# A convolution and attention trunk: the softmax statistics of the attention's second stage on ScalarE's DMA queue, and another order at its end

## Chip, core and metric

The kernel runs on one core of a Trainium2 chip. Its engines work in parallel, each through its own list of instructions in order: TensorE (PE in the profile, its weight loads PEld), VectorE (DVE), ScalarE (ACT), GpSimd (POOL) and SyncE (SP). SP, POOL and ACT can each start DMA transfers. The metric is the time of one execution on the device in microseconds (us); lower is better.

## What is computed

The reference is a trunk of two layers on an input of 1024 tokens by 1024 features, in float32. The first layer is a gated short convolution, the second an attention with three groups per head, dilated by 1, 4 and 16:

```
h = rms_norm(x, g);  proj = h @ w_in
for g, (window, dilation) in enumerate(((128, 1), (512, 4), (2048, 16))):
    q, k = rms_norm of this group's queries and keys; v
    o_g, lse_g = softmax(q k^T / 8 + bias) v          # causal, within the window, in residue classes
alpha = softmax over the three groups of lse_g
o = sum_g alpha_g * o_g
x = x + (o * silu(z)) @ w_out
```

There are 16 heads of 64 features; the kernel works on them as eight head pairs (`hp`). The point that matters here is `alpha`: the three groups of a head are merged by weights that come from their softmax maxima and denominators, for each token. These statistics are small, but each group holds its tokens in another order.

## The kernel before

Earlier stages compute the convolution layer and the projections, and leave queries, keys, values and the gate in DRAM (`qkd`, `vd`, `zd`). The second stage, from line 815 on, is the attention with the output projection. In it the order of every engine is the program's own: nothing is reordered.

A unit is one head pair and one group. Groups 0 and 1 are cut into four steps each, group 2 into two, so a head pair has ten steps and the stage 80. `make` gives each step its parts: `A` (line 893) computes scores in TensorE and, on VectorE, adds the bias and takes the negated maximum (into `nl`); `E` (line 940) takes the exponentials on ScalarE and their sums (into `nl` too); `B` (line 944) transposes the result in TensorE and copies it out of PSUM (`pts`), on VectorE or ScalarE; `C` (line 953) multiplies by the values, and the last `C` of a half calls `finish`, which copies the output `O`.

The main loop (line 1214) runs step numbers `k`. A part with lag `n` belonging to step `j` runs at `k = j + n`: `A` at lag 0, `B` at 2, `C` at 4. At each `k` the lags run in the order 0, 1, 4, 3, 5 to 16, 2; then come the exponentials of step `k` (key `"exps"`), then pieces of the output projection (`extra`), then loads and splits of weights (`begins`).

The last step of each unit (`end`) carries more. `store` (line 987) writes `nl` of groups 0 and 1 to DRAM (`nld`), and in group 2 reads both back as `ml`, in group 2's order of tokens: the trip through DRAM is how the order is changed. The stores consist of pieces of 16 bytes: 1024 in one DMA for group 0, 512 in each of two for group 1; the load is two DMAs of 64 rows of 256 bytes. `weights` (line 1000) takes the common maximum and the exponents' differences on VectorE and their exponentials on ScalarE; `shares` (line 1013) gives `alpha` (`fo`); `store_shares` (line 1026) writes it to DRAM (`fd`); `spread` (line 1030) reads it back, broadcast over the 64 features of a head, into `fb` or `sqacc`, two DMAs of 256 KB for each group. `scale` (VectorE) and `add` (GpSimd) merge the outputs; `gate`, `high` and `low` multiply by the gate and split the result into two parts for exact products. Before the change `store`, `store_shares` and `spread` are all issued by GpSimd, in its one queue, with the additions of `add` between them.

The output projection of head pairs 0 to 5 runs in pieces beside later steps (`some`, line 1162), each with a PSUM bank by name: `pd`, `po`, `pt` or `ps`. Its weights are loaded by `fetch` on SP and split into two parts by `split` (ScalarE) and `split_low` (VectorE). After step 80, pair 7's merging (`spread_last`, `last`) and the remaining products of pairs 6 and 7 end the kernel; five tiles of them (`first`) are begun before pair 7's result is there.

Of the kernel before, what the change touches and what calls it, by code (L numbers as in the profile page):

```python
# [28 lines left out]
HP = H // 2  # L29
# [6 lines left out]
def trunk(ctx: ExitStack, tc: tile.TileContext, a, out):  # L36
    nc = tc.nc
# [60 lines left out]
    def spread(hf, src, pool):  # L98
        cs = slice(hf * HALF, hf * HALF + HALF)
        pb = pool.tile([P, HALF], F32, name="st", tag="st")  # L100
        for j in range(4):
            b = hf * 4 + j
            nc.tensor.transpose(pb[:, j * P:(j + 1) * P], src[:, b:b + 1].to_broadcast([P, P]), ident)
        if src is rtok:
            nc.scalar.activation(R1[:, cs], pb, AF.Copy)
        else:
            mt = ftile()
            mc = mt.rearrange("p (c q) -> p c q", q=32)
            nc.vector.transpose(mc, pb.rearrange("p (c q) -> p c q", q=32))
            nc.vector.tensor_scalar(er2[:, hf * 16:(hf + 1) * 16], mc[:, :, 0], 8.0 * EPS, None, op0=OP.mult)  # L110
# [10 lines left out]
    nld = dram.tile([HP, S, 2, 4], F32, name="nld")  # L121
# [13 lines left out]
    with tc.tile_pool(name="wq", bufs=1) as wq, tc.tile_pool(name="sle", bufs=1) as sle, \  # L135
# [11 lines left out]
        def ftile():  # L147
            t = fp.tile([P, HALF], F32, name="f", tag="f", bufs=12)
            return t
# [185 lines left out]
        with tc.tile_pool(name="rp", bufs=1, side="right") as rp, tc.tile_pool(name="cp", bufs=2, side="right") as cp, \  # L335
# [62 lines left out]
            with tc.manual_schedule(engines={mybir.EngineType.Activation}):  # L398
                ps, T = {}, {}
# [107 lines left out]
        with tc.tile_pool(name="ev", bufs=1, side="right", reuse_waits="tile") as ev, tc.tile_pool(name="xb", bufs=1, side="right", reuse_waits="tile") as xb, \  # L507
# [35 lines left out]
            WO, ps = {}, {}  # L543
# [271 lines left out]
    with tc.tile_pool(name="sp", bufs=1, space=PSUM) as sp, tc.tile_pool(name="ptp", bufs=2, space=PSUM) as ptp, \  # L815
# [34 lines left out]
        def scores():  # L850
            turns[0] += 1
            return banks[turns[0] % 3]
# [11 lines left out]
        def attention(hp, g):  # L864

            u = {}
# [120 lines left out]
            def store():  # L987

                if g == 2:
                    u["ml"] = sm.tile([P, 8, 2, 4], F32, name="ml", tag="ml", bufs=1)  # L990
                    for a, hs in enumerate((lo, up)):
                        nc.gpsimd.dma_start(u["ml"][hs], nld[hp].rearrange("(i a r) g e -> a i r g e", a=2, r=8)[a])
                elif g == 0:
                    nc.gpsimd.dma_start(nld[hp, :, 0].rearrange("(b t) e -> t b e", b=8), u["nl"])
                else:
                    for n in range(2):
                        nc.gpsimd.dma_start(nld[hp, :, 1].rearrange("(n s c) e -> n s c e", n=2, c=4)[n],
                                            u["nl"][:, 4 * n:4 * n + 4])

            def weights():  # L1000
# [29 lines left out]
            def spread(w):  # L1030
                fb = u["fb", w] = fbp.tile([P, S], F32, name="fb", tag="fb") if w else sqacc
                for s, hs in enumerate((lo, up)):
                    nc.gpsimd.dma_start(fb[hs], fd[hp, w, s][None, :].to_broadcast([64, S]))

            def scale(w):
                nc.vector.tensor_tensor(O[hp, w], O[hp, w], u["fb", w], op=OP.mult)

            def add(w):
                nc.gpsimd.tensor_tensor(O[hp, 1], O[hp, 1], O[hp, w], op=OP.add)
# [22 lines left out]
            def spread_last(hf):  # L1062

                b0, b1, b2 = (scores().rearrange("p a b -> p (a b)") for _ in range(3))
                for w in (2, 1):
                    for r in range(8):
                        for a, b in enumerate((b0, b1)):
                            hs = slice(64 * a + 32 * hf, 64 * a + 32 * hf + 32)
                            nc.tensor.transpose(b.rearrange("p (w i r) -> p w r i", w=2, r=8)[:, w - 1, r],
                                                u["wide", w][hs, r * P:r * P + P], ident[hs, hs])  # L1070
                mine = ident.rearrange("p (a h i) -> p h a i", a=2, h=2)[:, hf]
                for r in range(8):
                    nc.tensor.matmul(b2.rearrange("p (i a r) -> p r a i", a=2, r=8)[:, r],
                                     u["wide", 0][:, r * P:r * P + P], mine, start=True, stop=True)
                u["fb", 0] = b2
                for w in (2, 1):
                    u["fb", w] = [b.rearrange("p (w i r) -> p w i r", w=2, r=8)[:, w - 1] for b in (b0, b1)]
# [19 lines left out]
            steps = []  # L1097
            for q in range(2):
                for js in ([[2 * q, 2 * q + 4, 2 * q + 1, 2 * q + 5]] if g == 2 else
                           [[4 * q, 4 * q + 1], [4 * q + 2, 4 * q + 3]]):  # L1100
                    st = make(js, not steps)
                    steps.append({lag: [f] for lag, f in zip((0, LB, LC, "exps"), st)})
            end = steps[-1]
            end.setdefault(1 if g < 2 else 2 if hp < 2 else 1 if hp < HP - 2 else 0, []).append(store)
            if g == 2:
                if hp == HP - 1:
                    steps[-2][3] = steps[-2].pop(LC)
                    end[3] = end.pop(LC)
                    todo = [(2, shares), (2, wide), (3, lambda: spread_last(0)), (3, lambda: last(0, 0)),
                            (3, lambda: last(0, 1))]  # L1110
                    ending.update(turn=end.pop(LB)[0], weights=weights, spread=spread_last, last=last)
                else:

                    todo = [(2, weights), (3, shares), (3, store_shares), (4, lambda: spread(2)),
                            (4, lambda: spread(1)), (4, lambda: spread(0)), (8, lambda: scale(2)),
                            (9, lambda: scale(1)), (9, lambda: add(2)), (10, lambda: scale(0)),
                            (10, lambda: add(0)), (12, gate), (12, high), (13, low)] if hp == HP - 2 else [
                            (4 if hp < 2 else 3, weights), (5, shares), (5, store_shares), (7, lambda: spread(2)),
                            (7, lambda: spread(1)), (7, lambda: spread(0)), (10, lambda: scale(2)),
                            (11, lambda: scale(1)), (11, lambda: add(2)), (12, lambda: scale(0)),  # L1120
                            (12, lambda: add(0)), (13, gate), (14, high), (15, low)]
                for lag, f in todo:
                    end.setdefault(lag, []).append(f)
# [30 lines left out]
        def bank(name):  # L1154
            if name in ("pd", "po"):
                return (pp1 if name == "pd" else opp).tile([P, HALF], F32, name=name, tag=name)
            t = scores() if name == "ps" else ptp.tile([P, 4, P], F32, name=name, tag=name)
            return t.rearrange("p a b -> p (a b)")
# [3 lines left out]
        def some(kts, dt, hf, name):  # L1162

            ps = bank(name)
            dense(ps, kts, dt, hf, True, True)
            sums.append((ps, acc[dt][:, half(hf)]))

        def add_sums():
            while sums:
                ps, x = sums.pop(0)  # L1170
                nc.vector.tensor_tensor(x, ps, x, op=OP.add)  # L1171

        steps, at = [], {}
# [7 lines left out]
        tiles = [(dt, hf) for hf in range(2) for dt in range(KT)]  # L1181

        def when(k, f, *x):
            begins.setdefault(k, []).append(lambda: f(*x))
# [7 lines left out]
        for r in range(3):  # L1192
            k0 = at[2 * r + 2, 0][0] + LD
            k = k0
            for i, (dt, hf) in enumerate(tiles):
                late = k >= len(steps)
                name = "pd" if not late else (("pd", "ps"), ("pd", "ps"), ("pd", "pt"), ("pt", "pd"))[
                    min(k - len(steps), 3)][i % 2]
                if i >= 14:
                    name = "po"  # L1200
                extra.setdefault(k, []).append(lambda r=r, dt=dt, hf=hf, name=name:
                                               some((2 * r, 2 * r + 1), dt, hf, name))
                k += (i % 2 if i < 13 else 0) if late else 1
        for kt in range(KT):
            k = (at[kt // 2 * 2 + 2, 0][0] + 4 if kt < 6 else len(steps) - 6) + 2 * (kt % 2)
            when(k - 5 - 2 * (kt % 2), fetch, kt)
            when(k, split, kt)
            when(k + 2, split_low, kt)
# [4 lines left out]
        k = 0  # L1213
# [22 lines left out]

        last = ending["last"]
        add_sums()
        first = [(dt, hf, bank(name)) for (dt, hf), name in zip(tiles, ("pt", "pt", "po", "po", "pd"))]
        for dt, hf, ps in first:  # L1240
            dense(ps, (6,), dt, hf, True, False)
        ending["spread"](1)
        last(1, 0)
        last(0, 2)
        for dt, hf, ps in first:
            dense(ps, (7,), dt, hf, False, True)
        last(1, 1)
# [3 lines left out]
        for dt, hf, ps in first[2:]:  # L1251
            close(ps, dt, hf)
        for i, (dt, hf) in enumerate(tiles[5:]):
            ps = bank(("ps", "ps", "ps", "pt", "pt", "po", "po", "pd", "ps", "ps", "ps")[i])
            dense(ps, (6, 7), dt, hf, True, True)
            close(ps, dt, hf)

# [66 lines left out]
```

## Time and profile before

| What | Value |
|---|---|
| Median of 3 runs | 1973.18 us (1970.7 to 1974.63) |
| Profiled execution | 1968.56 us |
| Its span, first to last instruction | 1966.8 us |
| Mean granted TensorE clock | 0.991 |
| TensorE busy | 1913.9 us, 97% |
| VectorE busy | 1495.3 us, 76% |
| ScalarE busy | 886.9 us, 45% |
| GpSimd busy | 847.6 us, 43% |

The times of the profile are those of one execution. A row of the timeline gives the start, the duration, the engine, the line of the code, the operation with what it writes and reads (`out<-in`) and, in brackets, how long the engine was idle before it and what ended that. A row of waits gives who waited for whom, then the sum in us, how often, and the longest. A row of a source line gives durations in ns as min/median/max. "DMA to landing" is the time from issue until the transfer's semaphore says that the data has arrived, again as min/median/max, for the line named before it. A row of stretches gives, for each engine, the busy time in that stretch.

### The profile page before, as it was taken

The page shows a single profiled execution, that of the slowest core. Times are in us where ns is not written, and L with a number is a line of the kernel's source. Part 1 is how long each engine was busy: PE and PEld are TensorE (multiplying, and loading weights), DVE is VectorE, ACT ScalarE, POOL GpSimd, SP SyncE. Part 2 cuts the span into 40 slices and gives each one's busy share as a digit, 9 for nine tenths or more (in the row PEclk, how much of TensorE's full clock was granted, in tenths as well). Part 3 has the DMA queues.
Part 4 walks back from the last instruction along what each step waited for, and adds up shares of the span by engine and source line. Part 5 has one row for each costly group of instructions (what it writes and reads, how often), then busy time and mean ns, then how long its engine had stood idle before and what let it go on. Part 6 is the DMA issues. An engine that isn't in the chain of part 4 may idle for free. (4 is left out here: it accounts for less than half of the span.)

```text
span 1966.8 us, 30588 instructions
## 1 busy us (share of the span) xinstructions
PE 1913.9 (97%) x10894; PEld 1555.4 (79%) x10894; DVE 1495.3 (76%) x2769; ACT 886.9 (45%) x2031; POOL 847.6 (43%) x767
## 2 busy tenths in 40 slices
PE   8999999999999999999999999999999999889988
PEld 6888888888888888878878888888888876667767
DVE  7876766666666655788888689868988878878896
ACT  6433333333334444443433443343344338877770
POOL 0366667666665211333434444444344441333230
PEclk9999999999999999999999999999999999999999
DMA  6312232222224665322323232333323247897742
GB/s 198 117 58 88 87 107 76 97 80 93 81 80 143 195 230 177 119 90 91 124 97 123 81 119 96 106 110 107 105 89 118 97 163 234 244 280 229 225 124 86
DMA packets 116777, 253.79 MB, mean 129 GB/s; under 512 B 17598, under 2 KB 22814, under 8 KB 116624
## 3 DMA queue, kind: packets, MB, share of 16 engines
q1 hardware_dynamic: 93280, 176.89, 27.9%
q0 software_dynamic: 23344, 74.95, 11.3%
q8 instruction: 85, 1.39, 0.3%
q14 instruction: 68, 0.56, 0.1%
HBM read 192.53 MB, written 67.64 MB: 132 GB/s over the span
## 5 line engine op out<-in xcount | busy, mean ns | idle before, releaser
L165 DVE TENSOR_TENSOR ws<-wr,ws 128x512 fp32r<-128x512 f32 x284 | 274.4, 968 | 120.8 <-ACT ws L164 119.3
L164 ACT ACTIVATE ws<-wr 128x512 fp32r<-128x512 f32 x284 | 178.3, 629 | 356.1 <-PE pp L304 231.9
L164 ACT ACTIVATE ws<-sr 128x512 fp32r<-128x512 f32 x272 | 169.9, 629 | 295.7 <-PE pp L304 240.6
L276 POOL TENSOR_TENSOR sr<-wr 128x512 f32<-128x512 f32 x136 | 185.6, 1365 | 264.2 <-DMA wr<-in_conv_w_in 67.5
L165 DVE TENSOR_TENSOR ws<-sr,ws 128x512 fp32r<-128x512 f32 x272 | 227.0, 842 | 71.6 <-ACT ws L164 69.4
L313 DVE TENSOR_TENSOR f<-pp,f 128x512 f32<-128x512 f32 x204 | 139.7, 685 | 93.0 <-PE pp L304 86.3
L942 ACT ACTIVATE xs<-xs,nl 128x256 f32<-128x256 f32 (+2 forms) x384 | 160.5, 424 | 1.0 <-DVE nl L936 1.0
L309 ACT ACTIVATE f<-pp 128x512 f32<-128x512 f32 x228 | 132.7, 582 | 27.4 <-POOL blkc L682 12.7
L671 ACT ACTIVATE f<-f 128x512 f32<-128x512 f32 x96 | 60.7, 632 | 138.7 <-DVE f L313 102.1
L276 POOL TENSOR_TENSOR sr<-wr,sr 128x512 f32<-128x512 f32 x68 | 88.5, 1302 | 70.3 <-issue 47.4
L936 DVE CUSTOM_DVE_ANT_0 xs<-ps,bt 128x256 f32<-128x256 f32 (+2 forms) x384 | 102.5, 325 | 12.5 <-PE ps L923 7.4
L301 PE MATMUL pp<-blkg,ws 128*128 128x512 f32 x272 | 107.2, 394 | 3.2 <-ACT f L309 3.2
L301 PE MATMUL pp<-blkf,ws 128*128 128x512 f32 x272 | 108.5, 399 | 0.7 <-ACT f L309 0.7
L301 PE MATMUL pp<-blkb,ws 128*128 128x512 f32 x272 | 108.1, 398 | 0.0
L301 PE MATMUL pp<-blka,ws 128*128 128x512 f32 x272 | 107.3, 394 | 0.7 <-ACT f L309 0.7
L301 PE MATMUL pp<-blkd,ws 128*128 128x512 f32 x272 | 106.9, 393 | 0.0
L304 PE MATMUL pp<-blkb,ws 128*128 128x512 f32 x272 | 106.6, 392 | 0.0
L303 PE MATMUL pp<-blkb,ws 128*128 128x512 f32 x272 | 106.5, 392 | 0.0
L304 PE MATMUL pp<-blkf,ws 128*128 128x512 f32 x272 | 106.3, 391 | 0.0
L276 POOL TENSOR_TENSOR sr<-sr,wr 128x512 f32<-128x512 f32 x68 | 104.0, 1529 | 4.9
L304 PE MATMUL pp<-blkd,ws 128*128 128x512 f32 x272 | 106.0, 390 | 0.0
L304 PE MATMUL pp<-blka,ws 128*128 128x512 f32 x272 | 106.0, 390 | 0.0
(341 smaller groups left out, 5280.5 us busy)
## 6 DMA issues: line engine op xcount, KB each, us to landing
wr<-in_conv_w_in SPq DMA_DIRECT2D x128, 256.0 KB, 3.1
wr<-in_wqk SPq DMA_DIRECT2D x96, 256.0 KB, 3.1
qkd<-blkc POOLq DMA_DIRECT2D x48, 512.0 KB, 3.4
qk<-qkd SPq DMA_DIRECT2D x48, 512.0 KB, 5.2
wr<-in_conv_w_out SPq DMA_DIRECT2D x64, 256.0 KB, 3.1
f<-in_x SPq DMA_DIRECT2D x48, 256.0 KB, 4.4
wr<-in_wv SPq DMA_DIRECT2D x48, 256.0 KB, 3.2
vd<-f POOLq DMA_DIRECT2D x48, 256.0 KB, 2.6
```

Of the source, the lines that this page charges most:

```text
L164: nc.scalar.activation(t[:, 0], src, AF.Copy)
L165: nc.vector.tensor_tensor(t[:, 1], src, t[:, 0].bitcast(F32), op=OP.subtract)
L276: nc.gpsimd.tensor_tensor(t, x, y, op=op)
L301: nc.tensor.matmul(ps, w[:, 0, ws], b[:, k, 0], start=new and k == 0, stop=False, skip_group_check=not new)
L303: nc.tensor.matmul(ps, w[:, 0, ws], b[:, k, 1], start=False, stop=False, skip_group_check=not new)
L304: nc.tensor.matmul(ps, w[:, 1, ws], b[:, k, 0], start=False, stop=end and k == 3, skip_group_check=not new)
L309: nc.scalar.activation(t, ps, AF.Copy)
L313: nc.vector.tensor_tensor(m, ps, m, op=OP.add)
L671: nc.scalar.activation(sq, t, AF.Square)
L936: nc.vector.tensor_tensor_reduce(out=x, in0=flat[s][:, cols], in1=u["bt"][s][:, bs], op0=OP.add, op1=OP.min, scale=-1.0, scalar=3e38, accu ...
L942: nc.scalar.activation(x, x, AF.Exp, bias=nm, scale=-1.0, accum_out=L)
```

## The change

Four things change. In `store` all DMAs go from GpSimd's queue to ScalarE's. `store` itself moves from lags 0 to 2 of the unit's last step to the place right behind that step's exponentials. In head pairs 0 and 1 `weights`, `shares`, `store_shares` and `spread` come one step earlier; in head pair 6 the scalings, the additions and the gate come one step earlier. At the end, the late pieces of the output projection use other banks, the last two weight rows are fetched and split two steps earlier, the five tiles begun first use the banks in another order, and the subtraction for the first half of pair 7, `last(0, 2)`, stands ahead of `last(1, 0)`.

```diff
                 if g == 2:
                     u["ml"] = sm.tile([P, 8, 2, 4], F32, name="ml", tag="ml", bufs=1)
                     for a, hs in enumerate((lo, up)):
-                        nc.gpsimd.dma_start(u["ml"][hs], nld[hp].rearrange("(i a r) g e -> a i r g e", a=2, r=8)[a])
+                        nc.scalar.dma_start(u["ml"][hs], nld[hp].rearrange("(i a r) g e -> a i r g e", a=2, r=8)[a])
                 elif g == 0:
-                    nc.gpsimd.dma_start(nld[hp, :, 0].rearrange("(b t) e -> t b e", b=8), u["nl"])
+                    nc.scalar.dma_start(nld[hp, :, 0].rearrange("(b t) e -> t b e", b=8), u["nl"])
                 else:
                     for n in range(2):
-                        nc.gpsimd.dma_start(nld[hp, :, 1].rearrange("(n s c) e -> n s c e", n=2, c=4)[n],
+                        nc.scalar.dma_start(nld[hp, :, 1].rearrange("(n s c) e -> n s c e", n=2, c=4)[n],
                                             u["nl"][:, 4 * n:4 * n + 4])
...
-            end.setdefault(1 if g < 2 else 2 if hp < 2 else 1 if hp < HP - 2 else 0, []).append(store)
+            end["exps"].append(store)
...
+                    w = 4 if hp < 2 else 5
                     todo = [(2, weights), (3, shares), (3, store_shares), (4, lambda: spread(2)),
-                            (4, lambda: spread(1)), (4, lambda: spread(0)), (8, lambda: scale(2)),
-                            (9, lambda: scale(1)), (9, lambda: add(2)), (10, lambda: scale(0)),
-                            (10, lambda: add(0)), (12, gate), (12, high), (13, low)] if hp == HP - 2 else [
-                            (4 if hp < 2 else 3, weights), (5, shares), (5, store_shares), (7, lambda: spread(2)),
-                            (7, lambda: spread(1)), (7, lambda: spread(0)), (10, lambda: scale(2)),
+                            (4, lambda: spread(1)), (4, lambda: spread(0)), (7, lambda: scale(2)),
+                            (8, lambda: scale(1)), (8, lambda: add(2)), (9, lambda: scale(0)),
+                            (9, lambda: add(0)), (11, gate), (12, high), (13, low)] if hp == HP - 2 else [
+                            (3, weights), (w, shares), (w, store_shares), (w + 2, lambda: spread(2)),
+                            (w + 2, lambda: spread(1)), (w + 2, lambda: spread(0)), (10, lambda: scale(2)),
...
-                name = "pd" if not late else (("pd", "ps"), ("pd", "ps"), ("pd", "pt"), ("pt", "pd"))[
-                    min(k - len(steps), 3)][i % 2]
-                if i >= 14:
-                    name = "po"
+                name = "pd"
+                if late:
+                    name = {5: "ps", 7: "ps", 9: "pt", 10: "pt", 11: "po", 12: "po", 14: "pt", 15: "pt"}.get(i, "pd")
...
-            k = (at[kt // 2 * 2 + 2, 0][0] + 4 if kt < 6 else len(steps) - 6) + 2 * (kt % 2)
+            k = (at[kt // 2 * 2 + 2, 0][0] + 4 if kt < 6 else len(steps) - 8) + 2 * (kt % 2)
...
-        first = [(dt, hf, bank(name)) for (dt, hf), name in zip(tiles, ("pt", "pt", "po", "po", "pd"))]
+        first = [(dt, hf, bank(name)) for (dt, hf), name in zip(tiles, ("po", "po", "pd", "pt", "pt"))]
         for dt, hf, ps in first:
             dense(ps, (6,), dt, hf, True, False)
         ending["spread"](1)
+        last(0, 2)
         last(1, 0)
-        last(0, 2)
...
-            ps = bank(("ps", "ps", "ps", "pt", "pt", "po", "po", "pd", "ps", "ps", "ps")[i])
+            ps = bank(("ps", "ps", "ps", "po", "po", "pd", "pt", "pt", "ps", "ps", "ps")[i])
```

## The prediction

> **What bounds the kernel now.** I read the page first, then, in the attention's second stage (from 1627 us, where the first score matmul starts, to the end), the waits of TensorE, its timeline with the idle time in brackets, the timelines of VectorE (DVE), GpSimd (POOL) and ScalarE (ACT) around each hole, and the busy time by stretch.
>
> ```profile
> span 1966.8 us, 30588 instructions
> PE 1913.9 (97%) x10894; PEld 1555.4 (79%) x10894; DVE 1495.3 (76%) x2769; ACT 886.9 (45%) x2031; POOL 847.6 (43%) x767
> ...
> PE pt L949 <- DVE pts L860: 16.0, 9, 5.5
> ...
> PE pd L1135 <- DVE acc L1171: 2.5, 2, 1.5
> ...
> PE pt L1136 <- DVE qk L1095: 1.1, 1, 1.1
> ```
>
> TensorE is the bound, and all that the change touches is holes of a few microseconds in the last 340. The largest group, 16.0 us, is transposes that wait for DVE to empty a PSUM bank (`pts`). The holes, one by one, are the next rows; the number in brackets is the idle time.
>
> ```profile
> 1681.28 0.44 PE L949 MATMUL pt<-ident,xs 128*128 128x128 f32 x2 [2.43 <-DVE pts L860]
> ...
> 1685.26 0.44 PE L949 MATMUL pt<-ident,xs 128*128 128x128 f32 x2 [1.16 <-DVE pts L860]
> ...
> 1689.86 0.90 PE L949 MATMUL pt<-ident,xs 128*128 128x128 f32 x3 [0.67 <-DVE pts L860]
> ...
> 1729.62 1.12 PE L949 MATMUL pt<-ident,xs 128*128 128x128 f32 x4 [5.53 <-DVE pts L860]
> ...
> 1908.38 0.50 PE L1135 MATMUL pd<-y,y 128*128 128x512 f32 x1 [1.55 <-DVE acc L1171]
> ...
> 1928.02 0.50 PE L1135 MATMUL pd<-y,y 128*128 128x512 f32 x1 [0.99 <-DVE acc L1171]
> ...
> 1942.93 0.54 PE L1136 MATMUL pt<-qk,y 128*128 128x512 f32 x1 [1.09 <-DVE qk L1095]
> ```
>
> DVE was late because it, working in order, itself stood still:
>
> ```profile
> 1679.39 1.23 DVE L1036 TENSOR_TENSOR o<-o,fb 128x1024 f32<-128x1024 f32 x1 [2.11 <-DMA fb<-fd]
> ...
> 1683.64 1.23 DVE L1036 TENSOR_TENSOR o<-o,fb 128x1024 f32<-128x1024 f32 x1 [1.31 <-DMA fb<-fd]
> ...
> 1688.24 1.23 DVE L1036 TENSOR_TENSOR o<-o,sqacc 128x1024 f32<-128x1024 f32 x1 [1.07 <-DMA sqacc<-fd]
> ...
> 1697.78 0.17 DVE L1006 TENSOR_TENSOR mx<-ml 128x16 f32<-128x16 f32 x1 [0.89 <-DMA ml<-nld]
> ...
> 1726.66 0.79 DVE L1006 TENSOR_TENSOR mx<-ml 128x16 f32<-128x16 f32 x1 [4.63 <-DMA ml<-nld]
> ...
> 1896.03 1.22 DVE L1149 TENSOR_TENSOR y<-wraw,y 128x1024 fp32r<-128x1024 f32 x1
> ...
> 1904.71 3.02 DVE L1149 TENSOR_TENSOR y<-wraw,y 128x1024 fp32r<-128x1024 f32 x1
> ```
>
> So head pair 0 waits for its spread shares, pairs 1 and 2 for `ml`. Why these land late is in POOL's queue:
>
> ```profile
> 1671.62 2.09 POOL L1033 DMA_DIRECT2D fb<-fd  x4 [4.21 <-PE po L970]
> ...
> 1674.72 1.56 POOL L997 DMA_DIRECT2D nld<-nl  x2
> ...
> 1691.91 1.08 POOL L992 DMA_DIRECT2D ml<-nld  x2
> ...
> 1712.03 0.73 POOL L997 DMA_DIRECT2D nld<-nl  x1 [1.62 <-ACT xs L942]
> ...
> 1721.54 1.08 POOL L992 DMA_DIRECT2D ml<-nld  x2 [8.79 <-DMA nld<-nl]
> 1722.62 4.79 POOL L1039 TENSOR_TENSOR o<-o 128x1024 f32<-128x1024 f32 x2
> ...
> 1904.27 2.37 POOL L1039 TENSOR_TENSOR o<-o 128x1024 f32<-128x1024 f32 x1 [1.25 <-DVE o L1036]
> ```
>
> The 8 KB store of group 1's maxima stands in one queue behind 1.5 MB of spread shares; POOL sits 8.79 us on its landing and can neither load `ml` nor add. The last two rows also show that DVE's L1149 took 3.02 in place of 1.22 us, until POOL's addition ended (1904.27 + 2.37).
>
> **Issues on ACT.** Per head pair five DMAs move from POOL to ACT, each right behind the exponentials that fill `nl`. Whoever issues on ACT holds the exponentials and bank copies queued behind. No DMA is issued on ACT before the change, so SP's rows bound it.
>
> ```profile
> L879 SPq DMA_DIRECT2D bt<-sk x32: 319/320/1340, 1605.3 to 1860.4; - x32
> ...
> L877 SPq DMA_DIRECT2D bt<-sk x32: 444/506/1367, 1625.4 to 1871.0; - x32
> ...
> 1631.00:1682.00 51.00, 45.81 (x715) 34.68 (x708) 41.66 (x223) 48.41 (x213) 10.38 (x16) 1.00 0.78 242
> 1682.00:1719.00 37.00, 30.70 (x442) 22.47 (x436) 32.59 (x139) 29.30 (x116) 12.62 (x15) 0.91 0.86 244
> 1719.00:1757.00 38.00, 31.65 (x404) 24.53 (x404) 27.77 (x118) 27.52 (x113) 12.83 (x16) 0.91 0.89 262
> 1757.00:1795.00 38.00, 37.98 (x468) 29.09 (x467) 35.29 (x135) 29.83 (x116) 12.90 (x16) 1.00 0.95 290
> ```
>
> Of one kind: 0.32 us at least (L879, 128 rows of 1 KB); 0.506 us for small scattered rows (L877, 64 of 256 B), the nearest to these stores, so I take it. In the first stretch, head pairs 0 and 1, ACT is busy 48.41 of 51 us (the columns: busy time of PE, weight load, DVE, ACT and POOL with counts, granted clock, DMA share, GB/s): eight issues there cost 8 x 0.506 = **+4.0**. Bounds: 0 (8 x 0.32 = 2.6, the whole of ACT's 2.6 idle); and, if the time grows with the pieces, 0.32 us / 128 = 2.5 ns each: a group-0 store of 1024 pieces 2.56 us, the two group-1 stores of 512 pieces 1.28 each, so 2 x 5.1 + 2 x 0.5 = +11.2. Later ACT idles 8 to 10 us in each 37 to 38 us, and the issues (2.5 us, at most 6.1 per pair) lie in it: 0, with the bounds -1 (POOL is free of them) and +3 (a copy late for its bank).
>
> **The added wait.** ACT must not issue `ml` before both stores of group 1 have landed; POOL bore this wait so far.
>
> ```profile
> L997 POOL DMA_DIRECT2D nld<-nl x16: 709/737/889, 1644.2 to 1902.3; - x16
> ...
> DMA to landing us min/median/max: 2.5/7.6/13.7
> 1674.32 0.19 ACT L942 ACTIVATION_READ_ACCUMULATOR xs<-xs,nl 128x1 f32 x1
> ...
> 1680.58 0.19 ACT L942 ACTIVATION_READ_ACCUMULATOR xs<-xs,nl 128x1 f32 x1
> ...
> 1718.28 0.20 ACT L942 ACTIVATION_READ_ACCUMULATOR xs<-xs,nl 128x1 f32 x1
> ml<-nld POOLq DMA_DIRECT2D x16, 16.0 KB, 4.6
> ```
>
> From the last exponential of pair 1's group 1 (1674.5) to that of its group 2 (1680.8) are 6.3 us. A landing of 7.6 us, the median on POOL's queue, leaves ACT 1.3 us to wait: twice, in pairs 0 and 1, **+2.6**. Bounds: 0 (2.5 us, the fastest landing), and 13.7 - 6.3 = 7.4 for pair 1, the rival below.
>
> The Trainium skill, "DMA: Bandwidth & Descriptors", section "Issuing engines are not separate DMA queues", speaks against the change: all issuers run on the same 16 engines, and another issuer saves only the time of issuing. The same page's "Queues, rings and completion order" says that each DMA engine takes turns between the queues' rings, packet by packet, which lets a store on an empty ring pass the spread shares. The 8.79 us of the POOL row above do not tell them apart, since store and shares were in one ring; by the first it is rival 3 and 1977.9, by the second the sum below holds, 1966.5.
>
> **What goes.** *Pair 0* (shares and spread one step earlier): DVE's waits of 2.11, 1.31 and 1.07 us add up to a lateness of 4.5. Steps last about 2.5 us there (51 us for 20), so some 2 us remain; of the 4.3 us of TensorE's three holes 2.3 go, and pair 1's 0.89 with an `ml` that is issued at 1682 and not at 1691: -3.2, and with a little of the half clock below **-3.5**; bounds -5.1 and -1. More than 4.4 isn't there: DVE's idle time in the second stretch (37 less 32.59), which is late next. *Pair 2*: pair 1's spread, a step earlier too, is out of the way by some 3 us, so the store from 1712 lands in about 6, `ml` goes at 1718.5, lands 4.6 later at 1723, and DVE, ready at 1722.0, waits 1 us instead of 4.63. POOL's additions (1722.62) no longer queue behind `ml`, so `mx` takes 0.2 and not 0.79 us. Of 5.53 us, 4.3 go; the bounds are -5.5 and 0. After such holes the granted clock (third figure from the right) was half:
>
> ```profile
> 1728.30:1735.00 6.70, 5.33 (x32) 4.37 (x32) 6.60 (x27) 4.10 (x11) 1.01 (x2) 0.50 0.54 171
> ...
> 1943.30:1946.60 3.30, 3.30 (x9) 2.60 (x8) 3.23 (x6) 0.63 (x1) 0.00 (x0) 0.50 0.06 24
> ```
>
> In the first of these DVE was the busier, so only 1 us of the half-clock time counts (0 to 3.3): pair 2 **-5.3**. Pairs 3 to 6 keep their lags: 0.
>
> *The end.* The splits of the last two weight rows two steps earlier take L1149 out of POOL's way: the hole of 1.55 goes. Their 1.22 us now share a step with pair 6's first scaling, which is also moved; SP's two `wraw` loads go two steps earlier past `bt` and `qk` loads, at no cost while those are prefetched. The late tiles' other banks remove the 0.99 (the second use of `pd` waits for an addition; `po` is free by then). The subtraction for the first half ahead of `last(1, 0)` removes the 1.09, and with it perhaps half-clock time, 3.3 / 2 = 1.65. Together 5.3; since the moved splits meet a full DVE I take **-4.5** (bounds -5.3 and -2).
>
> **Sum:** 4.0 + 2.6 - 3.5 - 5.3 - 4.5 = **-6.7 us**. The profiled execution took 1968.56 us (its span 1966.8); the median of the runs is 1973.18, 4.6 above it. From the median: **1966.5 us**; a profiled execution like the one shown would take 1961.9.
>
> **Rivals.**
> 1. *All is hidden* (0.15). The stores land in 2.5 us, ACT's idle time takes the issues: 0 - 5.1 - 5.5 - 3.3 - 5.3 = -19.2, 1954.0. For it: ACT idles 8 us and more in all later stretches. Against: not in the first.
> 2. *The pieces cost ACT time* (0.17): +11.2 in place of 4.0, so 0.5: 1973.7. For it: 1024 pieces of 16 B; against: L877 with half the rows takes longer than L879, so rows don't set it.
> 3. *Slower: ACT is blocked by the landing* (0.16). The shares still fill the DMA engines, stores on ACT's queue land in 13.7 us, the maximum on POOL's; in pair 1 ACT waits 7.4 in place of 1.3 (+6.1), in pair 2 `ml` comes as late as before (+5.3): -6.7 + 11.4 = +4.7, 1977.9. It decides from a landing of about 11 us: 3.4 us more than 7.6, counted in both pairs, use up the 6.7. For it: the DMA share is 0.78 to 0.95 in the stretches above. Against: pair 0's and 1's shares start a step earlier.
> 4. *It does not do what it says* (0.10): pairs 0 to 2 wait as long for their loads as before, so only the issues and the end stay: 4.0 - 4.5 = -0.5, 1972.7; with ACT's waits (+2.6) 1975.3.
>
> **Chances.** Forecast 0.42 (faster 0.36, same 0.06), rival 1 faster 0.15, rival 2 same 0.13 and slower 0.04, rival 3 slower 0.12 and same 0.04, rival 4 same 0.10: faster by over 0.2% (3.9 us, about what a measurement of this kernel can tell from no change) 0.51, same 0.33, slower 0.16. The range leaves out the far half of rival 1 and the worst of rivals 2 and 3: 1957 to 1978.
>
> **What would show it.** Issues on ACT: rows L992, L994 and L997 of ACT's queue near 0.5 us (over 1.2: rival 2). The wait: `ml`'s landing and ACT's idle time before the copies at about 1681 (over 4 us: rival 3). Pair 2: `mx` waiting 1 us or less. The end: no L1149 of 3 us and none of its three holes. Holes of TensorE on ACT before 1682 that sum to over 7 us would make the forecast wrong.

## The result: slower

| Kernel | Median of the runs | Lowest to highest | Ratio to before, 95% interval |
|---|---|---|---|
| before | 1973.06 us (6 runs) | 1966.59 to 1975.64 | |
| after | 1982.34 us (6 runs) | 1980.9 to 1988.24 | 1.0055 (1.0036 to 1.0073) |

The change costs 9.3 us where 6.7 us of gain were forecast, and the time lies above the range. The profiled execution after took 1988.24 us, the slowest of its six. Its page, the span, the busy time and the DMA queues (packets, MB, share of 16 engines):

```profile
span 1986.5 us, 30521 instructions
...
PE 1914.1 (96%) x10894; PEld 1554.9 (78%) x10894; DVE 1501.2 (76%) x2769; ACT 886.4 (45%) x2031; POOL 817.5 (41%) x727
...
q1 hardware_dynamic: 93280, 176.89, 27.7%
q0 software_dynamic: 22064, 74.42, 11.0%
q10 hardware_dynamic: 18048, 0.53, 0.6%
```

TensorE does the same work (1914.1 against 1913.9 us); what grew is its idle time. The changed stage alone, from its first score matmul to the end (TensorE's busy time is the third figure), before and then after:

```profile
1627.16:1966.80 339.64, 305.93 (x3729) 235.16 (x3728) 280.66 (x1075) 228.89 (x905) 94.18 (x112) 0.95 0.68 205
```

```profile
1630.95:1986.50 355.55, 305.79 (x3729) 235.34 (x3728) 274.74 (x1075) 227.70 (x905) 66.36 (x72) 0.94 0.67 195
```

The stage is 15.9 us longer, all of it idle time; 3.8 us more were lost ahead of it, where the program is the same. These 19.7 us between two profiled executions are twice the 9.3 us between the medians: the rows below show where the changed kernel loses in a long execution, and the medians say how much. `q10` is new: ScalarE's queue, with 0.53 MB in 18048 packets, 29 bytes each on average. Whom TensorE waits for, first before, then after, in the waits from 1623 us to the end (sum, times, longest):

```profile
PE pt L949 <- ACT pts L862: 2.1, 5, 0.5
```

```profile
PE pt L949 <- ACT pts L862: 27.2, 9, 10.4
PE pt L949 <- DVE pts L860: 8.7, 7, 3.8
```

The 16.0 us on VectorE's copies shrank to 8.7, and 27.2 us on ScalarE's copies came in their place. In TensorE's timeline after, these are four holes, in pairs 0, 1, 2 and 3:

```profile
1663.44 0.69 PE L949 MATMUL pt<-ident,xs 128*128 128x128 f32 x2 [3.58 <-ACT pts L862]
...
1702.35 1.12 PE L949 MATMUL pt<-ident,xs 128*128 128x128 f32 x4 [10.44 <-ACT pts L862]
...
1740.97 0.69 PE L949 MATMUL pt<-ident,xs 128*128 128x128 f32 x2 [4.00 <-ACT pts L862]
...
1784.17 1.11 PE L949 MATMUL pt<-ident,xs 128*128 128x128 f32 x4 [6.94 <-ACT pts L862]
```

ScalarE's timeline around the second of them shows why the copy is late:

```profile
1691.69 0.19 ACT L942 ACTIVATION_READ_ACCUMULATOR xs<-xs,nl 128x1 f32 x1
1700.71 1.15 ACTq L992 DMA_DIRECT2D ml<-nld  x2
1701.91 0.38 ACT L862 ACTIVATE pts<-pt 128x256 f32<-128x256 f32 x1 [10.03 <-issue]
```

Its last exponential of group 2 ends at 1691.9; then ScalarE stands 8.8 us in front of the load of `ml`, issues it, and only then makes the copy for which TensorE waits. The stores that it waits for, by their source line in the trace (ns of the issue as min/median/max; landing in us the same way):

```profile
L997 ACTq DMA_DIRECT2D nld<-nl x16: 552/570/617, 1650.7 to 1927.6; - x16
...
DMA to landing us min/median/max: 2.8/10.0/15.8
```

The longest, 15.8 us, is pair 1's second store, issued at 1684.9: it landed at 1700.7, when ScalarE went on. So rival 3 happened, in pair 1 at least. (In pair 3 the last store had landed at 1779.8, and ScalarE issued the second load of `ml` only at 1783.2; the experiments come to that.) By the trace the first packet of pair 1's two stores moved at 1688.6, 5.7 us after the first of them was issued; with longer pieces, in the run long_pieces below, it was 5.1 us, so the pieces are not the reason for this part, and what is stays open. The queues in the two microseconds before 1698 (packets, MB, share) show what the store met:

```profile
q1 hardware_dynamic: 242, 0.76, 97.9%
q10 hardware_dynamic: 242, 0.00, 7.4%
```

As many packets of SyncE's loads (3 KB on average) as of the store (16 bytes): that is what engines that take turns give, and a store of 512 pieces of 16 bytes then needs 512 turns over the 16 engines. The Trainium skill, "DMA: Bandwidth & Descriptors", section "Queues, rings and completion order", gives a turn a whole packet of typically 9 to 17 descriptors; of the turns the trace agrees, of the size it does not: here every piece is a packet of its own, 242 against 242.

### The profile page after: what moved, and what is told of

Read it like the earlier page. It is cut to its first block, busy times and chain, and to the rows that moved or that the text cites. A ratio compares the mean times of both kernels' runs of the same rounds, so it can differ in the third digit from the quotient of the medians.

```text
span 1986.5 us, 30521 instructions
## 1 busy us (share of the span) xinstructions
PE 1914.1 (96%) x10894; PEld 1554.9 (78%) x10894; DVE 1501.2 (76%) x2769; ACT 886.4 (45%) x2031; POOL 817.5 (41%) x727
## 2 busy tenths in 40 slices
DMA packets 133544, 253.78 MB, mean 128 GB/s; under 512 B 35006, under 2 KB 39582, under 8 KB 133392
## 3 DMA queue, kind: packets, MB, share of 16 engines
q10 hardware_dynamic: 18048, 0.53, 0.6%
## 5 line engine op out<-in xcount | busy, mean ns | idle before, releaser
L165 DVE TENSOR_TENSOR ws<-wr,ws 128x512 fp32r<-128x512 f32 x284 | 284.7, 1004 | 119.4 <-ACT ws L164 117.6
L949 PE MATMUL pt<-ident,xs 128*128 128x128 f32 x496 | 79.8, 295 | 37.0 <-ACT pts L862 27.2
```

The costliest lines, as they stand in the source:

```text
L165: nc.vector.tensor_tensor(t[:, 1], src, t[:, 0].bitcast(F32), op=OP.subtract)
L949: nc.tensor.transpose(pt[:, i], xs[s][:, c[i][0]], ident)
```

## Experiments

Each ran beside the kernel before on the same chip, in three sessions of four: the first four of the table, the next four, and the last three with nine. The kernel before had a median of 1973.0 us (28 runs), 1973.1 (12) and 1971.1 (29) in them, so runs of different sessions are compared by their ratio to it. The twelfth, nine, ran once, for its trace (1986.13 us, with 7 MB of loads put in at its start).

| Run | What differs | Median, us | Lowest to highest | Ratio to before, 95% |
|---|---|---|---|---|
| all_pool | after, stores and `ml` on GpSimd | 1964.42 | 1963.89 to 1968.41 | 0.995 to 0.9976 |
| ml_pool | after, `ml` alone on GpSimd | 1978.29 | 1975.08 to 1984.37 | 1.0022 to 1.0045 |
| long_pieces | after, long pieces | 1976.16 | 1973.66 to 1981.6 | 1.0015 to 1.0034 |
| end_only | before with the new end | 1966.49 | 1961.49 to 1971.15 | 0.9955 to 0.9977 |
| ml_act | after, stores on GpSimd | 1981.73 | 1977.19 to 1984.65 | 1.0032 to 1.0057 |
| dup_short | all_pool, stores once more on ScalarE | 1978.93 | 1976.06 to 1983.9 | 1.0019 to 1.0044 |
| ml_pool_long | ml_pool with long pieces | 1963.51 | 1961.99 to 1965.61 | 0.9943 to 0.9968 |
| weights_late | end_only, pair 2's weights later | 1965.2 | 1963.25 to 1968.89 | 0.9949 to 0.9974 |
| dup_long | dup_short with long pieces | 1966.32 | 1964.3 to 1972.74 | 0.9958 to 0.9986 |
| bare_act | all_pool, two idle loads on ScalarE | 1978.29 | 1974.78 to 1980.68 | 1.0018 to 1.0043 |
| mix | all_pool, pairs 1 and 2 otherwise | 1968.95 | 1963.92 to 1973.77 | 0.9969 to 0.9996 |

### The queue, undone (all_pool)

```diff
-            end["exps"].append(store)
+            end.setdefault(1 if g < 2 or hp < HP - 2 else 0, []).append(store)
...
-                        nc.scalar.dma_start(u["ml"][hs], ...
+                        nc.gpsimd.dma_start(u["ml"][hs], ...
```

and the same for the three stores; earlier weights, earlier shares and the new end stay. The place changes with the queue: stores and load come a step after the exponentials (in pairs 6 and 7 the load at lag 0).

> The changed kernel with stores and load back on GpSimd's queue (ml one step after the unit's end, for pair 6 and 7 at its start); the earlier shares and the new end stay. Theory 'wait' (ScalarE stands still at ml until the stores have landed): all of TensorE's waits on ScalarE's copies over 3 us go, what is left of the change is the end (-4) and the earlier shares (-2 to -4), so 1965 to 1969, below the kernel before. Rival 'rest' (the earlier steps, banks or splits cost the time): it stays above 1978.

1964.42 us: 17.9 us under the changed kernel and 8.6 under the one before. Issuing on ScalarE, right behind the exponentials, is the whole loss; queue and place are undone together here. What is left of the waits, of TensorE and then of VectorE:

```profile
PE pt L949 <- DVE pts L860: 16.3, 6, 6.3
...
PE pt L949 <- ACT pts L862: 2.6, 7, 0.5
```

```profile
DVE mx L1006 <- DMA ml<-nld: 14.1, 4, 5.2
```

The holes on ScalarE are gone. But the sum on VectorE is that of before, 16.3 against 16.0 us. Before, VectorE waited for the spread shares in pair 0, and for `ml` twice, 5.5 us; now it waits for `ml` four times, 14.1 us. Weights that come a step earlier find no `ml`, though in pairs 0 and 1 its load comes a step earlier than before, too.

### The new end alone (end_only)

The kernel before with the banks, the splits, the order of `last`, and pair 6's earlier scalings, additions and gate from the change, nothing else.

> The kernel before with the new end alone (banks, splits two steps earlier, pair 6's scalings one earlier, the subtraction first). The forecast's term: -4.5, so 1967 to 1970, and none of the holes of 1.55, 0.99 and 1.09 us. Rival: the moved splits and scalings meet a full VectorE around step 76 and give it back: within 1.5 us of the kernel before.

1966.49 us, 6.5 under before (the interval of the ratio is 4.5 to 8.9 us). Against it all_pool, which adds the earlier weights, shares and `ml`, has 2.1 us less, but the two intervals of the ratio nearly coincide, so a gain of the earlier steps is not shown. Of the three holes of 1.55, 0.99 and 1.09 us none is left in this run's timeline of TensorE from 1905 us on. The splits of the weights are no longer stretched (1.21 us here), as VectorE's timeline of the changed kernel shows beside the 3.02 us of before:

```profile
1916.17 1.22 DVE L1150 TENSOR_TENSOR y<-wraw,y 128x1024 fp32r<-128x1024 f32 x1
...
1922.87 1.22 DVE L1150 TENSOR_TENSOR y<-wraw,y 128x1024 fp32r<-128x1024 f32 x1
```

### Only the load of `ml` back on GpSimd (ml_pool)

```diff
-                        nc.scalar.dma_start(u["ml"][hs], ...
+                        nc.gpsimd.dma_start(u["ml"][hs], ...
...
-            end["exps"].append(store)
+            if g == 2:
+                end.setdefault(1 if hp < HP - 2 else 0, []).append(store)
+            else:
+                end["exps"].append(store)
```

> The changed kernel with only the load of ml on GpSimd; the three stores per pair stay on ScalarE, so ScalarE still issues 24 of 40 DMAs and the landing stays slow (median near 10 us), but GpSimd bears the wait. Theory 'wait': no wait of TensorE on ScalarE's copies over 1 us; VectorE waits for ml in pairs 1 and 2 instead (2 to 8 us); time 1966 to 1976. Rival 'issue' (ScalarE's issues and the small pieces' traffic cost the time, wherever the wait is): above 1978.

1978.29 us: a miss for the theory that ScalarE's wait for the landing is all. ScalarE no longer stands (TensorE waits 3.3 us for it), yet 14 us more are used than in all_pool, and the time is that of the rival (small pieces' traffic or the issues). The stores still land late, and now VectorE waits longer and TensorE for VectorE (16.3 us in all_pool). The landing of L997, then VectorE's wait and TensorE's:

```profile
DMA to landing us min/median/max: 3.1/10.3/14.3
```

```profile
DVE mx L1006 <- DMA ml<-nld: 17.4, 4, 9.0
```

```profile
PE pt L949 <- DVE pts L860: 24.4, 9, 10.1
```

### Long pieces (long_pieces) and both at once (ml_pool_long)

```diff
-    nld = dram.tile([HP, S, 2, 4], F32, name="nld")
+    nld = dram.tile([HP, P, 64], F32, name="nld")
...
-                    nc.scalar.dma_start(nld[hp, :, 0].rearrange("(b t) e -> t b e", b=8), u["nl"])
+                    nc.scalar.dma_start(nld[hp, :, 0:32], u["nl"].rearrange("p a b -> p (a b)"))
...
```

Here the statistics stay in the order of their own group: the exchange of order is left out.

> The changed kernel with the same DMAs on the same queue at the same places, but the stores and the load move 128 or 64 rows as they stand (pieces of 128, 64 and 256 bytes), so the change of the tokens' order is left out. Theory 'turns' (on ScalarE's hardware queue each 16-byte piece takes a turn of its own against packets of the other queues): stores land in 3 to 6 us, ScalarE hardly waits, 1964 to 1972. Rival 'busy' (the landing is long because the DMA engines are busy with the shares, whatever the pieces): median landing stays near 10 us, ScalarE waits as long, above 1978.

1976.16 us, between the two theories. The landing of L997 got shorter, but ScalarE still stood before its copies:

```profile
DMA to landing us min/median/max: 1.4/6.3/9.8
```

```profile
ACT pts L862 <- DMA bt<-sk: 14.2, 2, 7.9
```

What ended these waits, by the trace, is the landing of `bt`, a load on SyncE's queue with which neither `ml` nor the copy has anything to do. That was the first sign of a second cause. With long pieces and `ml` on GpSimd's queue both are nearly gone (ScalarE waits once for `bt`, 1.4 us):

> Stores on ScalarE's queue in contiguous pieces of 128 and 64 bytes, the load of ml on GpSimd's queue in contiguous pieces of 256: both suspected losses taken away at once. The change of order between key groups is left out, so the shares are computed from other queries' sums. If landing and blocking are all there is: stores land in about 6 us, ml is issued 3 to 5 us earlier than with all on GpSimd in pairs 1 and 2, and the time is 1958 to 1965. If the issues on ScalarE cost by themselves: 1968 to 1974, with neither engine waiting for ml.

1963.51 us, as low as with all on GpSimd. So three stores a pair on ScalarE's queue cost nothing on balance if they are in long pieces and nobody on ScalarE waits. It is a balance: TensorE waits 4.8 us for ScalarE's copies against 2.6 in all_pool, and 11.9 for VectorE's against 16.3, since `ml` comes sooner (VectorE waits 4.2 us for it, not 14.1).

### Only the load of `ml` on ScalarE (ml_act)

The counterpart of ml_pool: the stores on GpSimd at lag 1, `ml` on ScalarE behind the exponentials.

> The changed kernel with the three stores of each head pair back on GpSimd's queue, a step after their exponentials; only the load of ml stays on ScalarE's, right behind the exponentials of group 2. 'Landing' (the stores' slow way on ScalarE's queue is the loss; which engine waits for it matters little): stores land in 7 to 8 us at the median again, 1964 to 1969. 'Blocked' (an in-order ScalarE that stands still costs more than a GpSimd that does, whoever stores): ScalarE waits 5 to 8 us in pairs 1 to 3 for a store that was issued a step later, TensorE's waits for ScalarE's pts sum to 12 to 20 us against 2.6 with all on GpSimd, 1972 to 1982.

1981.73 us, nearly all of the loss, though the stores land in 7.3 us at the median again. ScalarE's timeline in pairs 1 and 3:

```profile
1700.39 2.01 ACTq L992 DMA_DIRECT2D ml<-nld  x2
1702.50 0.38 ACT L862 ACTIVATE pts<-pt 128x256 f32<-128x256 f32 x1 [12.56 <-DMA ml<-nld]
...
1778.68 1.10 ACTq L992 DMA_DIRECT2D ml<-nld  x2
1779.89 0.38 ACT L862 ACTIVATE pts<-pt 128x256 f32<-128x256 f32 x1 [11.90 <-DMA acc<-x1d]
```

By the trace, pair 1's stores had landed at 1696.8 and pair 3's at 1770.9. ScalarE stood 3.6 and 7.8 us longer before its first load of `ml`, and in pair 3 the landing that ended it is that of `acc<-x1d`, SyncE's load of the residual. The trace names the semaphore by which each transfer tells that it has landed: in this stage the transfers of SyncE and ScalarE use the same eight in turn, and those of GpSimd eight others.

### A wait for nothing (bare_act)

```diff
+            def bare():
+                for i in range(2):
+                    nc.scalar.dma_start(scrap[hp, i], a["attn_norm"])
...
+            if g == 2:
+                end["exps"].append(bare)
             end.setdefault(1 if g < 2 or hp < HP - 2 else 0, []).append(store)
```

Added to all_pool: two loads of 4 KB from an input to a tensor that nobody reads.

> All small transfers on GpSimd's queue, and on ScalarE's, at the place where the changed kernel loads ml, two loads of 4 KB that need nothing and that nobody reads. 'Eight in flight' (ScalarE's issue waits for a load of SyncE's that went eight transfers before): ScalarE stands still there 2 to 8 us in pairs 1 to 3, with a load of SyncE's as the releaser, 1967 to 1974. 'Only its own data' (ScalarE waited for the stores alone): no hole, 1964 to 1966.

1978.29 us: these loads alone take the ratio to before from all_pool's 0.9963 to 1.0031, some 13 us. ScalarE's timeline, then TensorE's wait (a new line above them makes the copy L863 and the transposes L950):

```profile
1696.48 3.07 ACTq L1003 DMA_DIRECT2D scrap<-in_attn_norm  x2
1699.66 0.38 ACT L863 ACTIVATE pts<-pt 128x256 f32<-128x256 f32 x1 [8.79 <-DMA scrap<-in_attn_norm]
...
1774.27 2.69 ACTq L1003 DMA_DIRECT2D scrap<-in_attn_norm  x2
1777.07 0.38 ACT L863 ACTIVATE pts<-pt 128x256 f32<-128x256 f32 x1 [11.13 <-DMA scrap<-in_attn_norm]
```

```profile
PE pt L950 <- ACT pts L863: 23.3, 9, 8.8
```

An issue takes 0.5 us here; of the 8.79 and 11.13 us in which ScalarE made no copy, some 1.1 are the two issues, and the rest it stood for transfers that depend on nothing. In this run's stage 216 transfers of SyncE and ScalarE have a known landing of the one before them on the same semaphore; none was issued before that landing, and 49 within 0.1 us after it. Each of the 216 has that semaphore among those that it waits for, so the wait is one of the program. This is the second cause: each issue waits for the transfer before it on its semaphore, in 212 of the 216 the one eight places earlier, here a large load of SyncE's.

### The eight in flight, by themselves (nine)

```diff
...
+        for i in range(7):
+            nc.sync.dma_start(big[i], a["wqk"][i, 0])
+        for i in range(3):
+            nc.scalar.dma_start(tiny[i], a["attn_norm"])
...
```

The rest is all_pool.

> The version with all small transfers on GpSimd's queue, and at its very start, before anything else, seven loads of 1 MB on SyncE's queue and then three of 4 KB on ScalarE's, all from inputs into scratch tensors that nobody reads: nothing depends on anything. Only the moments of issue count, not the time. 'Eight in flight' (the transfers that SyncE and ScalarE issue share eight completion semaphores in turn, and each issue waits until the transfer before it on its semaphore has landed): the first small one is issued at once, the second only when SyncE's first load has landed, some 5 to 20 us later, the third when its second has. 'Separate': all three within 2 us.

As written, this missed: the three small transfers went at once, since the semaphores had been handed out to both queues by turns, and all three were among the first. The wait appeared on SyncE instead, as its timeline shows, with the row for ScalarE's three behind it:

```profile
8.07 0.49 SPq L47 DMA_DIRECT2D big<-in_wqk  x1
8.61 0.58 SPq L79 DMA_DIRECT2D conv_norm<-in_conv_norm  x1
11.04 0.33 SPq L181 DMA_DIRECT2D f<-in_x  x1
```

```profile
0.74 1.88 ACTq L49 DMA_DIRECT2D tiny<-in_attn_norm  x3
```

The trace has the first large load landing at 8.06, ScalarE's second small one at 8.42, the second large one at 11.02. From 4.3 us on eight were under way, six large and two small; the seventh large one, of the same input and with a place of its own, went at 8.07, when the first had landed. What came next on SyncE, at 8.61, had ScalarE's small transfer before it on its semaphore; but that had landed at 8.42, before SyncE was done with the issue at 8.07, so this run does not show that a transfer of ScalarE's holds SyncE. The next does.

### The stores twice (dup_short, dup_long)

```diff
+                if g == 0:
+                    nc.scalar.dma_start(nld2[hp, :, 0].rearrange("(b t) e -> t b e", b=8), u["nl"])
...
+            end["exps"].append(double)
             end.setdefault(1 if g < 2 or hp < HP - 2 else 0, []).append(store)
```

All on GpSimd, and each store once more on ScalarE's queue, for nobody: in pieces of 16 bytes, and in pieces of 128 and 64.

> The version with all small transfers on GpSimd's queue, and beside them each of the three stores once more on ScalarE's queue into a scratch tensor that nobody reads: the issues and the packets of 16 bytes without anyone waiting for their landing. 'Landing or blocked' (only the wait for a landing costs): 1964 to 1968, the issues at 1.5 us a pair lying in ScalarE's idle time except in pairs 0 and 1 (+2 to 3). 'Contention' (8192 more packets of 16 bytes per group slow everything that moves, or the issues on ScalarE cost by themselves): 1972 or more, with later landings of the store on GpSimd's queue and of the shares.

> As with the three stores once more on ScalarE's queue beside those on GpSimd's, but the copies on ScalarE's in contiguous pieces of 128 and 64 bytes: the same issues and semaphores, an eighth and a quarter of the packets. 'Short pieces' (packets of 16 bytes, and their slow landings, are what costs): 1964 to 1968, against 1978.9 with pieces of 16 bytes. 'Issues or semaphores': 1972 or more.

1978.93 us with short pieces, 1966.32 with long ones. The issues and the places among the eight are the same in both, so the short pieces make the difference; the copies land in 12.9 us at the median and 17.3 at most when short (group 1), in 7.1 and 12.2 when long. For dup_short, SyncE's waits (L878 and L843 load `bt` and `V`), then the landing of the real stores on GpSimd's queue (L998):

```profile
SPq L878 <- DMA nld<-nl: 12.1, 6, 3.2
...
SPq L843 <- DMA nld<-nl: 10.0, 3, 6.4
```

```profile
DMA to landing us min/median/max: 2.3/8.0/13.1
```

SyncE stood 22 us for stores that it does not need (1.2 in dup_long), so a slow transfer of ScalarE's also holds SyncE. The real stores landed little later: 8.0 us at the median and 13.1 at most, against 7.3 and 10.9 in all_pool, but 7.6 and 13.0 in dup_long. TensorE's waits for ScalarE grew by 4.5 us against all_pool, where an issue waited for a load of SyncE's, and those for VectorE's copies and maxima by 7.5, where `ml` came later. How these divide between the extra packets and the held loads was not separated.

### Two tries at a better version (weights_late, mix)

> The kernel before with the new end, and the weights of pair 2 one step later, as those of pairs 0 and 1 have been. 'In order' (the hole of 5.5 to 6.3 us in front of pair 2's last transposes comes because VectorE stands at mx, waiting for ml, with a bank's copy queued behind): the copy goes first, the hole shrinks to under 2 us, 1961 to 1964. 'Late anyway' (the bank would come free no sooner): 1966 to 1968, as with the new end alone.

> A try at a better version: all small transfers on GpSimd's queue, the earlier weights and shares kept for pair 0 alone, pairs 1 and 2 with the weights one step later than that and the shares at the place of before. The hole of 6.3 us in pair 1 (VectorE at mx, waiting for ml) shrinks to 3 to 4, pair 2's 4.4 stays: 1961 to 1964. If VectorE only stands elsewhere, waiting for the spread shares: 1964 to 1966.

Both missed. With pair 2's weights a step later (1965.2 us, not to be told from the new end alone) the hole of 5.5 us stays: VectorE then stands behind GpSimd's addition, up to 5.1 us, instead of at `mx`. TensorE's timeline and VectorE's wait:

```profile
1731.55 1.11 PE L949 MATMUL pt<-ident,xs 128*128 128x128 f32 x4 [5.53 <-DVE pts L860]
```

```profile
DVE sz L1042 <- POOL o L1039: 5.9, 2, 5.1
```

mix (1968.95, a ratio of 0.9983) is no better than all_pool (0.9963). Of the versions that compute everything, weights_late (0.9961), all_pool and end_only (0.9966) cannot be told apart: 0.34 to 0.39% under before, and the new end alone gives nearly all of it.

## Why the prediction was wrong

It summed 6.6 for ScalarE's queue, -8.8 for the earlier weights and shares, and -4.5 for the end. The runs give 17.9 (all_pool to after), -2.1 (end_only to all_pool) and -6.5 (end_only). These three add up to the measured 9.3 whatever the causes, since each starts where the next one ends; they say which terms were off: ScalarE's queue by 11.3, the earlier steps by 6.7, the end by -2.0.

- **The added wait (+2.6): the step that failed.** It took the 7.6 us of GpSimd's queue as the landing and argued that turns between queues might make it shorter. On ScalarE's queue it became longer, 10.0 at the median and 15.8 in pair 1, since each piece of 16 bytes takes a turn of its own; in long pieces the same stores on the same queue land in 6.3, and 9.8 at most. ScalarE then waited 8.8 us in pair 1 and not 1.3, and pairs 2 and 3, which counted nothing for it, had holes of 4.0 and 6.9 us too. The sign that was to give this away, holes on ScalarE before 1682 us of over 7, was set too early: 4.1 us lie there, and the hole of 10.4 ends at 1702.
- **What was not thought of:** a transfer on ScalarE also waits for the one before it on its semaphore, mostly one of SyncE's eight places earlier. bare_act shows this alone to be worth some 13 us. The stores on ScalarE's queue, with no load of `ml` there, cost 14 (ml_pool); how much of that is the late landing is open, since dup_short loses as much though the computation waits for none of its copies. Both at once cost 17.9, not 27: the two waits run side by side. In pairs 1 and 2 of the changed kernel the last store landed at 1700.7 and 1739.1, and SyncE's load that comes before one of the two `ml` loads on its semaphore at 1700.3 and 1738.8; in pair 3 the load came 3.4 us after the store.
- **Issues (+4.0):** right in kind. The rows of L994, L997 and L992 have medians of 0.364, 0.570 and 0.512 us, so a pair costs 0.364 + 2 x 0.570 + 2 x 0.512 = 2.5 us. The 1024 pieces take less time to issue than 512 in L997's form: rival 2 falls. dup_long adds three issues a pair, of 0.33 us each, and stays within 2 us of all_pool by the medians. What the issues cost in time was not measured by itself.
- **Pairs 0 and 2 (-3.5 and -5.3):** the waits for spread shares went in all_pool, as argued, but VectorE met `ml` instead, 14.1 us. The step wrongly let `ml` keep up with weights that come earlier; its chain of store, landing, load and landing did not get shorter. In the changed kernel pair 2's stores landed in 14.2 and 13.5 us where it had taken about 6. all_pool tests these terms with the stores on GpSimd; with the stores landing sooner on ScalarE's queue (ml_pool_long) the time is still only 2 to 3 us under end_only.
- **The end (-4.5):** right in its mechanism, since the three holes went; -6.5 was measured, beyond the bound of -5.3, with an interval from -4.5 to -8.9. One reading was loose: the stretched L1149 ended at 1907.7, 1.1 us after POOL's addition (1906.6) and not with it.
- **Rival 3** had the right mechanism on one side, the landing. It priced 13.7 us where 15.8 were measured, and only pairs 1 and 2. Of the two rules of the Trainium skill in the prediction, that of the issuing engines led to 1977.9, the nearer one; the rule of turns held in the trace, and led the wrong way because the size of a turn was not asked.

## What to carry to other kernels

Before a transfer is moved to another engine, ask three things: what stands behind its issue on that engine in order, which other transfers must land before it may be issued at all (here those of the engine that shares its semaphores), and into how many packets the new queue cuts it. An engine whose copies feed TensorE should issue no transfer that may wait; an issue itself is cheap (0.3 to 0.6 us), its waits are not. And when a consumer is moved earlier, see first that what it reads comes earlier too.

## What the runs showed that was not expected

- SyncE's and ScalarE's transfers of this program share eight semaphores. At most eight are in flight, and an issue waits for the landing of the one before it on its semaphore, mostly eight places earlier: two loads without any dependence kept ScalarE from its copies for 8.79 and 11.13 us.
- ScalarE's queue sends each piece of 16 bytes as a packet of its own: the packets under 512 bytes rose from 17598 before to 35006 after, by 17408, which is eight pairs of 2048 pieces and 128 rows. GpSimd's queue had joined them: its trace before has 256 packets of 512 bytes and 384 of 1024, after the change none, and they make up just what the stores and loads of `ml` move.
- The same bytes in the same number of transfers: 1978.93 us in pieces of 16 bytes, 1966.32 in pieces of 64 and 128, though nothing was computed from them.
